# A two-layer hybrid diffusion step on one core: mLSTM decay matrices built with the value blocks, and the layer norm's residual on another engine, traced later, with the layer norm at higher priority

## The chip, the cores and the metric

The kernel runs on one core of one Trainium2 chip. The metric is device microseconds of one execution, the median of the runs shown; lower is better. The engines are named as in the profile: PE (TensorE; PEld is its weight load), DVE (VectorE), ACT (ScalarE), POOL (GpSimd) and SP (SyncE, which here only issues transfers).

## The reference

Two token streams of 128 tokens and 1024 channels, a context (s = 0) and a sample (s = 1), go through the same two layers. A layer is a half-step SwiGLU feed-forward, a mixer and another half-step feed-forward. Each of these six sub-layers ends in a layer norm over a residual sum:

```python
f1 = _swiglu(x * (1.0 + sc1) + sh1, ffn1_w_gate, ffn1_w_up, ffn1_w_down)
x = _layer_norm(alpha * x + 0.5 * g1 * f1, ln_g, ln_b)
y, new_st = _mixer(x * (1.0 + sc2) + sh2, st, l, p)
x = _layer_norm(alpha * x + g2 * y, ln_g, ln_b)
```

The mixer runs gated linear attention (GLA, 4 heads) and an mLSTM (4 heads), each forward and backward, and merges them. The part of the mLSTM that the change touches is the decay matrix of each direction and head, and the factor of the carried state:

```python
log_d = where(mask, cum[..., :, None] - cum[..., None, :] + ic[..., None, :], -inf)
m_t = maximum(cum + m, log_d.max(-1))
d = exp(log_d - m_t[..., None])
inter = exp(cum + m - m_t)
s = einsum('bhtd,bhsd->bhts', q, k) * d
```

## The kernel before

All weights are fp32 and stream once from HBM. A `Block` is one 128x512 result per stream; it is cut into units of up to four 128-row weight tiles. For each half unit a 128x1024 tile `raw` is loaded, ACT rounds it to `hi` (L303) and DVE forms `lo = raw - hi` (L304), and PE adds three products, `hi·xh`, `lo·xh` and `hi·xl` (L319 to L321). `raw` has six buffers, `hi` and `lo` seven each, so a half unit's `hi` can be made only when PE has used an older one.

The main loop (L1047) takes one unit a turn: it loads the next unit, consumes unit i for stream 0 and unit i - 2 for stream 1 (`LAG = 2`), and adds a few conditioning matmuls. A block's `pre` runs before its first matmul of a stream, its `post` after its last.

The program is traced in that order, and a scheduler of the kernel's framework fixes each engine's queue when the kernel is compiled. It goes through the program on a clock of its own, and on each engine takes, of the instructions that are ready there, the one traced first. `issue_after(ins)` puts instructions behind `ins` on its engine, and `high_priority(offset=n)` ranks instructions as if they had been traced n earlier. On the chip each queue then runs strictly in that order. Most large tiles share one pool, `s4`, of 21 slots; they take slots in the order of tracing, so a tile traced late can't be made before those ahead of it have had theirs.

At the end of a sub-layer `ln_half` (two per stream: `y = acc·gate`, `y = alpha·x + y`, statistics; L377 to L381) and `ln_finish` run: mean and variance (L392), `rstd` on DVE and a power on POOL (L386), the normalised `y` (L398), eight transposes on PE, the modulated `mf` on DVE and ACT (L352, L354), and its split into `xh` (ACT) and `xl` (DVE, L332), which the next sub-layer's first matmuls need. The residual stream itself, `x = y·g + b`, is four POOL instructions of 128x512 for each stream (L404, L405); it is next read at the end of the following sub-layer.

In the mixer, `chain` (L531) is called ahead of stream 1's first unit. It makes the gates' running maxima, stores them (`Gd`), loads them back as rows spread over all partitions (`Db`, four transfers of 256 KB, L583), and at once makes the factors `ib` (ACT, eight exponentials, L588) and the decay matrices of both streams (DVE, 16 instructions, L592; ACT, two exponentials of 128x1024, L594). They are first used by block `q0`, the blocks' order being `v0 v1 k0 n0 k1 n1 r0 q0 ...` of two units each.

Of the kernel before, what the change touches and what calls it, by code (L numbers as in the profile page):

```python
# [12 lines left out]
AF = mybir.ActivationFunctionType  # L13
ALU = mybir.AluOpType
# [3 lines left out]
D = 1024  # L18
KT = D // 128
# [8 lines left out]
C_GG, C_GM = 7216, 8240  # L28
LAG = 2
SLOTS = 21  # L30


@with_exitstack
def hybrid_step(ctx: ExitStack, tc: tile.TileContext, I, O, n_sub=6):
# [21 lines left out]
    def s4(name, shape, dt=F32):  # L56
        return s4_p.tile([128] + shape, dt, name=name, tag="s4")
# [219 lines left out]
    def add_block(b, step=4):  # L277
        k0 = 0
        while k0 < b.nk:
            n = min(step, b.nk - k0)  # L280
            units.append((b, k0, n, {}, phase[0]))
            k0 += n

    def load(u, part=None):
        b, k0, n, w, _ = u
        for h in range(0, n, 2):
            if part == 1:
                raw = w.pop("raw")
                split_w(raw, w, h)
                continue  # L290
            raw = raw_p.tile([128, 2, 512], F32, name="raw", tag="raw")
            for src, c0, nn in b.srcs:
                nc.sync.dma_start(raw[:, :, c0:c0 + nn],
                                  src[128 * (k0 + h):128 * (k0 + h + 2), :].rearrange("(k p) n -> p k n", p=128))
            if part == 0:
                w["raw"] = raw
            else:
                split_w(raw, w, h)
# [71 lines left out]
    def ln_half(s, n, acc, fac):  # L370
        if n == 0:
            yt[s] = s4("y", [D])
            bst[s] = sm("bst", 12)
        sl = slice(512 * n, 512 * n + 512)
        y = yt[s]
        if fac == 1.0:
            V.tensor_tensor(y[:, sl], acc, gbc[s][:, sl], ALU.mult)  # L377
        else:
            V.scalar_tensor_tensor(y[:, sl], acc, fac, gbc[s][:, sl], ALU.mult, ALU.mult)
        V.scalar_tensor_tensor(y[:, sl], x[s][:, sl], ALPHA, y[:, sl], ALU.mult, ALU.add)  # L380
        V.bn_stats(bst[s][:, 6 * n:6 * n + 6], y[:, sl])  # L381
# [7 lines left out]
    def ln_finish(s, l, sub):  # L389
        y = yt.pop(s)  # L390
        mv = sm("mv", 2)
        V.bn_aggr(mv, bst.pop(s).rearrange("p (a b) -> p a b", b=6))  # L392
        r = rstd_of("rstd", mv[:, 1:2], 1.0, LN_EPS)
        idx = l * 3 + sub
        if idx + 1 < n_sub:
            for n in range(2):
                sl = slice(512 * n, 512 * n + 512)
                V.tensor_scalar(y[:, sl], y[:, sl], mv[:, 0:1], r, ALU.subtract, ALU.mult)  # L398
        if idx + 1 < n_sub:
            l2, sub2 = divmod(idx + 1, 3)  # L400
            modulate(s, y, l2, sub2)
            for n in range(2):
                sl = slice(512 * n, 512 * n + 512)
                G.tensor_tensor(x[s][:, sl], y[:, sl], lnbc["g"][:, sl], ALU.mult)  # L404
                G.tensor_tensor(x[s][:, sl], x[s][:, sl], lnbc["b"][:, sl], ALU.add)  # L405
        else:
            for n in range(2):
                sl = slice(512 * n, 512 * n + 512)
                V.scalar_tensor_tensor(y[:, sl], y[:, sl], mv[:, 0:1], lnbc["g"][:, sl], ALU.subtract, ALU.mult)
                V.scalar_tensor_tensor(x[s][:, sl], y[:, sl], r, lnbc["b"][:, sl], ALU.mult, ALU.add)  # L410
                nc.sync.dma_start(O["y_prompt" if s == 0 else "y_sample"][0, :, sl], x[s][:, sl])


    def ffn(l, sub, wg, wu, wd):
        sg, hid = {}, {}

        def xin(s, k):
            return xh[s][:, k, :], xl[s][:, k, :]

        def hidden(s, h, j, nt):  # L420
            pt = ms("hT", [4, 128])
            for t in range(nt):
                T.transpose(pt[:, t, :], h[:, 128 * t:128 * (t + 1)], ident)  # L423
            ht = s4("hid", [2, 4, 128], F32R) if nt == 4 else hb_p.tile([128, 2, 2, 128], F32R, name="hidb", tag="hidb")
            hid[s, j] = ht
            split_fm(ht[:, 0, 0:nt, :], ht[:, 1, 0:nt, :], pt[:, 0:nt, :])

        def gate_post(s, acc):
            sg[s] = t2("sg", [512])
            A.activation(sg[s], acc, AF.Silu)  # L430

        def up_post(j):
            def f(s, acc):
                h = sg.pop(s)
                V.tensor_tensor(h, h, acc, ALU.mult)
                hidden(s, h, j, 4)
            return f

        def mix_post(s, acc):
            h = t2("sg", [256])  # L440
            A.activation(h, acc[:, 0:256], AF.Silu)
            V.tensor_tensor(h, h, acc[:, 256:512], ALU.mult)
            hidden(s, h, 5, 2)

        for j in range(5):
            sl = slice(512 * j, 512 * j + 512)
            step = 2 if j == 0 and l == 0 and sub == 0 else 4
            add_block(Block(KT, [(wg[:, sl], 0, 512)], xin, gate_post), step)
            add_block(Block(KT, [(wu[:, sl], 0, 512)], xin, up_post(j)), step)
            if step == 2:  # L450
                units[:] = [units[4 * (i % 2) + i // 2] for i in range(8)]
        add_block(Block(KT, [(wg[:, 2560:2816], 0, 256), (wu[:, 2560:2816], 256, 256)], xin, mix_post))

        def hin(s, k):
            t = hid[s, k // 4]
            return t[:, 0, k % 4, :], t[:, 1, k % 4, :]

        def down_post(n):
            def f(s, acc):
                ln_half(s, n, acc, 0.5)  # L460
                if n == 1:
                    ln_finish(s, l, sub)
            return f

        for n in range(2):
            add_block(Block(KF, [(wd[:, 512 * n:512 * n + 512], 0, 512)], hin, down_post(n),
                            pre=(lambda s: ln_prefetch(s, l, sub)) if n == 0 else None))


    def mixer(l):  # L470
# [60 lines left out]
        def chain():  # L531
# [44 lines left out]
            A.activation(en, mt, AF.Exp, scale=-1.0)  # L576
            gd = dr_p.tile([128, 128], F32, name="Gd", tag="Gd")
            nc.sync.dma_start(gd, Gr)
            for s in range(2):
                Db = st["D", s] = s4("Db", [2, 4, 128])  # L580
                for d in range(2):
                    r = 32 * (2 * s + d)
                    nc.sync.dma_start(Db[:, d], gd[r:r + 4, :].unsqueeze(0).to_broadcast([128, 4, 128]))  # L583
                if s == 1:
                    ib = st["ib"] = s4("ib", [2, 4, 128])
                    for d in range(2):
                        for h in range(4):
                            A.activation(ib[:, d, h, :], Db[:, d, h, :], AF.Exp, scale=-1.0,  # L588
                                         bias=m0bc[l][:, 4 * d + h:4 * d + h + 1])
                for d in range(2):  # L590
                    for h in range(4):
                        V.scalar_tensor_tensor(Db[:, d, h, :], Db[:, d, h, :], gpad[:, s, d, h:h + 1],  # L592
                                               mk[:, 6 + d, :], ALU.subtract, ALU.max)
                A.activation(Db, Db, AF.Exp, scale=-1.0)  # L594
            Q.dma_start(O["m"][0, l, 0:1, :], m4[127:128, 0, 0, :])
            Q.dma_start(O["m"][0, l, 1:2, :], m4[0:1, 1, 0, :])


        vg, on = {}, {}
# [165 lines left out]
        def vm_post(n):  # L765
            def f(s, acc):
                if n == 0:
                    vm[s] = s4("vm", [4, 257])
                    G.memset(vm[s][:, :, 256:257], 1.0)
                A.activation(vm[s][:, 2 * n:2 * n + 2, 0:256], acc.rearrange("p (a b) -> p a b", a=2), AF.Copy)  # L770
            return f
# [100 lines left out]
        def col(c, n=512):  # L872
            return [(W[:, c:c + n], 0, n)]
# [7 lines left out]
                            xin, gla_post(pr), pre=gla_pre(pr)))  # L881

        def b_n(n):
            add_block(Block(KT, col(C_VM + 512 * n), xin, vm_post(n)))

        def b_q(h):
            add_block(Block(KT, [(W[:, C_QKM + 256 * h:C_QKM + 256 * h + 256], 0, 256),
# [60 lines left out]

        def out_post(n):
            def f(s, acc):  # L950
                ln_half(s, n, acc, 1.0)
                if n == 1:
                    ln_finish(s, l, 1)
            return f

        for n in range(2):
# [90 lines left out]
    for i in range(s0, n + LAG):  # L1047
        ahead = units[i + 1] if i + 1 < n else None
        if ahead and not last(i - LAG):
            load(ahead)  # L1050
        if i < n:
            consume(0, units[i])
        if i - LAG >= s0:
            consume(1, units[i - LAG])
        if ahead and last(i - LAG):
            with tc.issue_after(fin["V", 0, 0]), tc.issue_after(fin["A", 0, 0]):
                load(ahead)
        if i < n:
            for a in due[i]:
                ada_unit(*a)  # L1060
# [87 lines left out]
```

## Time and profile before

| | us |
|---|---|
| median of 3 runs | 1630.68 (1630.48 to 1632.51) |
| the profiled execution | 1633.1 |
| its span, first to last instruction | 1631.2 |
| PE busy in the span | 1584.0 (97%) |
| DVE busy | 978.9 (60%) |
| ACT busy | 757.4 (46%) |
| POOL busy | 117.9 (7%) |
| mean granted clock of PE | 0.991 |

The profiled execution is 1.9 us longer than its span and 2.4 us longer than the median. Ends of matmuls are modelled, so a busy PE is not a PE at its peak; where PE shows idle time, it had nothing to do. The six sub-layers end at about 250, 640, 850, 1045, 1425 and 1623 us of the span.

### The profile page before, as it was taken

The numbers are of one execution on the slowest core, as the hardware profiler recorded it, in microseconds if no ns is written. First come the engines' busy times: TensorE is split into PE (matmuls) and PEld (weight loads), VectorE is DVE, ScalarE is ACT, GpSimd is POOL, SyncE is SP. The second block draws the span as 40 slices with busy tenths as digits, with TensorE's granted clock in tenths as the row PEclk, the third lists the DMA queues.
The fourth block names the chain that finished last, engine by engine and source line by source line (L and its number), as shares of the span: only waits on it lengthen the run. The fifth ranks groups of instructions, "written<-read, shape, count | busy, mean of one in ns | idle before, by whom it ended". The sixth has DMA issues, their size and how long they took to land.

```text
span 1631.2 us, 20327 instructions
## 1 busy us (share of the span) xinstructions
PE 1584.0 (97%) x7323; PEld 1192.0 (73%) x7323; DVE 978.9 (60%) x1607; ACT 757.4 (46%) x1096; POOL 117.9 (7%) x142
## 2 busy tenths in 40 slices
PE   7999999899999999999999999989999999999997
PEld 3676676677677677777777888767777777768886
DVE  3544458557666558645565555666577665765555
ACT  2443334555565534444444444355556554454441
POOL 2000004000000002100011000220000000120000
PEclk9999999999999999999999999999999999999999
DMA  9777876665775785666855667576556766756671
GB/s 325 250 266 258 309 232 210 207 215 171 256 232 182 272 284 167 216 218 205 282 189 157 181 182 246 164 214 212 182 183 195 252 193 233 217 161 182 181 236 65
DMA packets 195982, 350.20 MB, mean 215 GB/s; under 512 B 17516, under 2 KB 73596, under 8 KB 195880
## 3 DMA queue, kind: packets, MB, share of 16 engines
q1 hardware_dynamic: 195320, 348.68, 66.3%
q8 instruction: 58, 0.95, 0.2%
q0 software_dynamic: 384, 0.13, 0.1%
q14 instruction: 44, 0.36, 0.1%
q10 hardware_dynamic: 176, 0.07, 0.0%
HBM read 341.30 MB, written 7.54 MB: 214 GB/s over the span
## 4 chain that ended last, share of the span: by engine, by line
PE 57%; issue 30%; DVE 6%; DMA 3%; ACT 2%; POOL 1%; SPq 0%; DVEq 0%; POOLq 0%; ACTq 0%
PE acc L319 15%; PE acc L320 15%; PE acc L321 15%; PE adaps L167 3%; DVE lo L304 2%; DMA Db<-Gd 1%; PE cfin L846 1%; PE hT L423 1%; DVE xl L332 1%; DMA araw<-in_w_ada 1%; POOL rstd L386 1%; PE num L818 1%; PE num L821 1%; ACT hi L303 1%; PE rg L798 0%
## 5 line engine op out<-in xcount | busy, mean ns | idle before, releaser
L304 DVE TENSOR_TENSOR lo<-raw,hi 128x1024 fp32r<-128x1024 f32 x456 | 559.5, 1229 | 366.5 <-ACT hi L303 363.7
L303 ACT ACTIVATE hi<-raw 128x1024 fp32r<-128x1024 f32 x456 | 480.9, 1059 | 426.4 <-PE acc L321 394.9
L319 PE MATMUL acc<-hi,xh 128*128 128x512 f32 x1280 | 517.2, 406 | 12.7 <-ACT xh L330 7.0
L321 PE MATMUL acc<-hi,xl 128*128 128x512 f32 x1280 | 515.0, 403 | 5.6 <-DVE xl L332 5.4
L320 PE MATMUL acc<-lo,xh 128*128 128x512 f32 x1280 | 514.2, 402 | 2.8 <-DVE lo L304 2.8
L319 PEld LDWEIGHTS acc<-hi,xh 128*128 128x128 f32 x1280 | 242.1, 189 | 110.8 <-issue 27.9
L321 PEld LDWEIGHTS acc<-hi,xl 128*128 128x128 f32 x1280 | 243.0, 190 | 63.5 <-DVE xl L332 9.5
L320 PEld LDWEIGHTS acc<-lo,xh 128*128 128x128 f32 x1280 | 242.8, 190 | 59.0 <-DVE lo L304 7.4
L319 PE MATMUL acc<-hi,hid 128*128 128x512 f32 x320 | 127.0, 397 | 0.0
L320 PE MATMUL acc<-lo,hid 128*128 128x512 f32 x320 | 126.6, 396 | 0.0
L321 PE MATMUL acc<-hi,hid 128*128 128x512 f32 x320 | 126.4, 395 | 0.0
L167 PE MATMUL adaps<-araw,condp 128*32 128x512 f32 x512 | 78.7, 604 | 0.0
L319 PEld LDWEIGHTS acc<-hi,hid 128*128 128x128 f32 x320 | 60.1, 188 | 18.7 <-issue 3.4
L320 PEld LDWEIGHTS acc<-lo,hid 128*128 128x128 f32 x320 | 60.1, 188 | 14.4 <-issue 0.8
L321 PEld LDWEIGHTS acc<-hi,hid 128*128 128x128 f32 x320 | 60.2, 188 | 13.9
L386 POOL TENSOR_TENSOR rstd<-rstd,mhalf 128x1 f32<-128x1 f32 x12 | 13.9, 1158 | 777.0 <-DVE rstd L385 661.0
L330 ACT ACTIVATE hid<-hT 128x512 fp32r<-128x512 f32 x40 | 24.0, 599 | 85.8 <-PE hT L423 85.7
L319 PE MATMUL acc<-hi,oh 128*128 128x512 f32 x128 | 51.2, 400 | 0.0
L320 PE MATMUL acc<-lo,oh 128*128 128x512 f32 x128 | 51.2, 400 | 0.0
L321 PE MATMUL acc<-hi,ol 128*128 128x512 f32 x128 | 50.5, 395 | 0.0
L386 POOL TENSOR_TENSOR hr<-hr,mhalf 128x1 f32<-128x1 f32 x32 | 17.9, 560 | 422.5 <-DVE hr L385 362.9
L430 ACT ACTIVATE sg<-acc 128x512 f32<-128x512 f32 x40 | 23.9, 598 | 46.4 <-PE acc L321 46.4
(246 smaller groups left out, 1539.6 us busy)
## 6 DMA issues: line engine op xcount, KB each, us to landing
araw<-in_w_ada SPq DMA_DIRECT2D x128, 512.0 KB
raw<-in_w_in SPq DMA_DIRECT2D x96, 512.0 KB
raw<-in_ffn_w_down SPq DMA_DIRECT2D x88, 512.0 KB
raw<-in_ffn_w_gate SPq DMA_DIRECT2D x80, 512.0 KB
raw<-in_ffn_w_up SPq DMA_DIRECT2D x80, 512.0 KB
raw<-in_w_in SPq DMA_DIRECT2D x96, 256.0 KB
araw<-in_w_ada SPq DMA_DIRECT2D x32, 256.0 KB
raw<-in_w_br_gla SPq DMA_DIRECT2D x16, 512.0 KB
```

Source lines behind the costliest of these rows:

```text
L167: T.matmul(ps[32 * q:32 * q + 32, :], lhsT=condp[:, k, :], rhs=raw[q], start=(k == 0), stop=(k == KT - 1), tile_position=(0, 32 * q))
L303: A.activation(hi, raw, AF.Copy)
L304: V.tensor_tensor(lo, raw, hi.bitcast(F32), ALU.subtract)
L319: T.matmul(acc, lhsT=xh, rhs=wh, start=(k == 0), stop=False)
L320: T.matmul(acc, lhsT=xh, rhs=wl, start=False, stop=False)
L321: T.matmul(acc, lhsT=xl, rhs=wh, start=False, stop=(k == b.nk - 1))
L330: a = A.activation(dst_h, src, AF.Copy, scale=scale)
L332: v = V.tensor_tensor(dst_l, src, dst_h.bitcast(F32), ALU.subtract)
L386: G.tensor_tensor(r, r, mhalf[:, 0:1], ALU.pow)
L423: T.transpose(pt[:, t, :], h[:, 128 * t:128 * (t + 1)], ident)
L430: A.activation(sg[s], acc, AF.Silu)
L818: T.matmul(num, lhsT=sT[:, d, :], rhs=vh, start=True, stop=(s == 0))
```

## The change

There are two parts. In the mixer, `chain` keeps only the store of `Gd`; the loads of a stream's rows move to the `pre` of block `n0`, and `ib` and the decay matrices of that stream to the `pre` of block `n1`. At the ends of sub-layers, `ln_half` and `ln_finish` are traced with a priority 100 higher, and the residual becomes two DVE instructions of 128x1024 for each stream, traced at the end of the second turn after the one in which `ln_finish` ran and put behind the last `xl` of that stream on DVE's queue. The number and size of all other instructions stay.

```diff
+PRIO = 100
...
             modulate(s, y, l2, sub2)
-            for n in range(2):
-                sl = slice(512 * n, 512 * n + 512)
-                G.tensor_tensor(x[s][:, sl], y[:, sl], lnbc["g"][:, sl], ALU.mult)
-                G.tensor_tensor(x[s][:, sl], x[s][:, sl], lnbc["b"][:, sl], ALU.add)
+            later.append([3, s, y, lnbc["g"], lnbc["b"], fin["V", s, 1]])
...
+    later = []
+
+    def residuals():
+
+        for e in later:
+            e[0] -= 1
+        while later and later[0][0] <= 0:
+            _, s, y, g, b, behind = later.pop(0)
+            with tc.issue_after(behind):
+                V.tensor_tensor(x[s], y, g, ALU.mult)
+                V.tensor_tensor(x[s], x[s], b, ALU.add)
...
-                ln_half(s, n, acc, 0.5)
-                if n == 1:
-                    ln_finish(s, l, sub)
+                with tc.high_priority(offset=PRIO):
+                    ln_half(s, n, acc, 0.5)
+                    if n == 1:
+                        ln_finish(s, l, sub)
...
             nc.sync.dma_start(gd, Gr)
-            for s in range(2):
-                Db = st["D", s] = s4("Db", [2, 4, 128])
-                for d in range(2):
-                    r = 32 * (2 * s + d)
-                    nc.sync.dma_start(Db[:, d], gd[r:r + 4, :].unsqueeze(0).to_broadcast([128, 4, 128]))
...
+            st["gd"] = gd
...
+        def rows_load(s):
+            Db = st["D", s] = s4("Db", [2, 4, 128])
+            for d in range(2):
+                r = 32 * (2 * s + d)
+                nc.sync.dma_start(Db[:, d], st["gd"][r:r + 4, :].unsqueeze(0).to_broadcast([128, 4, 128]))
+
+        def decays(s):
+            mk, Db = st["mk"], st["D", s]
+            if s == 1:
+                ib = st["ib"] = s4("ib", [2, 4, 128])
                 for d in range(2):
                     for h in range(4):
+                        A.activation(ib[:, d, h, :], Db[:, d, h, :], AF.Exp, scale=-1.0,
+                                     bias=m0bc[l][:, 4 * d + h:4 * d + h + 1])
+            for d in range(2):
+                for h in range(4):
+                    V.scalar_tensor_tensor(Db[:, d, h, :], Db[:, d, h, :], gpad[:, s, d, h:h + 1],
+                                           mk[:, 6 + d, :], ALU.subtract, ALU.max)
+            A.activation(Db, Db, AF.Exp, scale=-1.0)
...
         def b_n(n):
-            add_block(Block(KT, col(C_VM + 512 * n), xin, vm_post(n)))
+            add_block(Block(KT, col(C_VM + 512 * n), xin, vm_post(n), pre=(rows_load, decays)[n]))
...
+        residuals()
         if i < n:
             for a in due[i]:
                 ada_unit(*a)
```

`out_post` of the mixer gets the same `high_priority` as `down_post`.

## Rows read from the trace of the kernel before

**Rows 1.** The page, part 1: busy time, share of the span, instructions.

```profile
PE 1584.0 (97%) x7323; PEld 1192.0 (73%) x7323; DVE 978.9 (60%) x1607; ACT 757.4 (46%) x1096; POOL 117.9 (7%) x142
```

**Rows 2.** Windows: stretch, length, busy us (instructions) by engine, granted clock, DMA share, GB/s.

```profile
250.00:275.00 25.00, 22.84 (x119) 15.73 (x118) 20.33 (x38) 10.96 (x19) 16.88 (x13) 1.00 0.69 225
295.00:300.00 5.00, 3.85 (x19) 2.84 (x17) 2.23 (x9) 0.56 (x2) 0.00 (x0) 1.00 0.96 219
300.00:305.00 5.00, 1.64 (x5) 1.30 (x6) 2.33 (x8) 5.00 (x12) 0.00 (x0) 0.89 0.73 281
305.00:310.00 5.00, 5.00 (x20) 3.25 (x18) 0.93 (x1) 3.83 (x9) 0.00 (x0) 0.77 0.00 0
385.00:400.00 15.00, 15.00 (x78) 12.14 (x78) 11.18 (x25) 10.22 (x16) 0.53 (x1) 1.00 0.46 142
635.00:660.00 25.00, 21.09 (x95) 15.51 (x94) 21.68 (x34) 13.55 (x20) 14.87 (x10) 1.00 0.48 149
850.00:855.00 5.00, 1.60 (x4) 0.84 (x5) 5.00 (x6) 4.96 (x8) 4.04 (x3) 0.84 0.14 53
855.00:860.00 5.00, 5.00 (x13) 3.84 (x13) 4.56 (x8) 0.25 (x1) 1.46 (x1) 0.50 0.43 110
860.00:865.00 5.00, 5.00 (x27) 4.26 (x26) 2.40 (x6) 1.88 (x4) 4.61 (x4) 0.98 0.58 208
1045.00:1070.00 25.00, 21.97 (x111) 15.61 (x110) 20.34 (x38) 10.48 (x19) 17.47 (x13) 1.00 0.55 185
1090.00:1095.00 5.00, 2.27 (x13) 1.62 (x12) 2.74 (x9) 2.31 (x6) 0.00 (x0) 1.00 1.02 199
1095.00:1100.00 5.00, 5.00 (x20) 4.05 (x19) 1.52 (x5) 4.41 (x10) 0.00 (x0) 0.66 1.05 381
1420.00:1445.00 25.00, 20.99 (x95) 15.46 (x94) 21.71 (x33) 13.37 (x20) 15.36 (x10) 1.00 0.46 147
```

**Rows 3.** Waits of 284:310 us: who waited for whom, total, times, longest.

```profile
ACT ib L588 <- DMA Db<-Gd: 5.5, 1, 5.5
...
PE acc L319 <- ACT vg L605: 4.5, 1, 4.5
```

**Rows 4.** Waits of 1080:1100 us.

```profile
ACT ib L588 <- DMA Db<-Gd: 2.9, 1, 2.9
PE argA L657 <- DVE lal L332: 2.7, 1, 2.7
```

**Rows 5.** Tile Db: duration ns min/median/max, first and last start, forms.

```profile
L592 DVE SCALAR_TENSOR_TENSOR Db<-Db,gpad,mk x32: 343/350/354, 294.8 to 1096.2; 128x128 f32<-128x128 f32 x32
L588 ACT ACTIVATE ib<-Db,m0bc x16: 385/387/402, 299.4 to 1095.8; 128x128 f32<-128x128 f32 x16
...
L594 ACT ACTIVATE Db<-Db x4: 1040/1050/1062, 300.6 to 1096.6; 128x1024 f32<-128x1024 f32 x4
```

**Rows 6.** Timeline of VectorE, 842:860 us: start, length, instruction, idle before.

```profile
844.60 1.21 DVE L304 TENSOR_TENSOR lo<-raw,hi 128x1024 fp32r<-128x1024 f32 x1
...
845.84 1.17 DVE L304 TENSOR_TENSOR lo<-raw,hi 128x1024 fp32r<-128x1024 f32 x1
...
851.22 1.69 DVE L380 SCALAR_TENSOR_TENSOR y<-x,y 128x512 f32<-128x512 f32 x1
852.83 1.76 DVE L332 TENSOR_TENSOR xl<-mf,xh 128x512 fp32r<-128x512 f32 x1
...
856.24 0.68 DVE L332 TENSOR_TENSOR xl<-mf,xh 128x512 fp32r<-128x512 f32 x1
```

**Rows 7.** Line L405 (residual on GpSimd): duration ns min/median/max.

```profile
L405 POOL TENSOR_TENSOR x<-x,lnbbc x20: 1272/1297/2253, 254.3 to 1443.7; 128x512 f32<-128x512 f32 x20
```

**Rows 8.** The page, part 5: instruction, count, busy us, mean ns, idle before it.

```profile
L304 DVE TENSOR_TENSOR lo<-raw,hi 128x1024 fp32r<-128x1024 f32 x456 | 559.5, 1229 | 366.5 <-ACT hi L303 363.7
```

**Rows 9.** Timeline of VectorE, 902:911 us, inside a feed-forward layer.

```profile
909.20 1.22 DVE L304 TENSOR_TENSOR lo<-raw,hi 128x1024 fp32r<-128x1024 f32 x1 [2.98 <-ACT hi L303]
```

**Rows 10.** Timeline of GpSimd, 0:4 us.

```profile
1.26 0.75 POOL L120 DMA_DIRECT2D m0bc<-in_state_mlstm_m  x1 [0.81 <-POOLq L1133]
```

More of the change, by code (lines that the diff above doesn't have):

```diff
@@ L578, in chain @@
             nc.sync.dma_start(gd, Gr)
-            for s in range(2):
-                Db = st["D", s] = s4("Db", [2, 4, 128])
-                for d in range(2):
-                    r = 32 * (2 * s + d)
-                    nc.sync.dma_start(Db[:, d], gd[r:r + 4, :].unsqueeze(0).to_broadcast([128, 4, 128]))
[L584 to L589, printed above, removed]
+            st["gd"] = gd
+            Q.dma_start(O["m"][0, l, 0:1, :], m4[127:128, 0, 0, :])
+            Q.dma_start(O["m"][0, l, 1:2, :], m4[0:1, 1, 0, :])
+        def rows_load(s):
[7 more added lines that the diff above has]
+                ib = st["ib"] = s4("ib", [2, 4, 128])
                 for d in range(2):
                     for h in range(4):
[L592 to L596, printed above, removed]
+                        A.activation(ib[:, d, h, :], Db[:, d, h, :], AF.Exp, scale=-1.0,
[5 more added lines that the diff above has]
+            A.activation(Db, Db, AF.Exp, scale=-1.0)
         vg, on = {}, {}
@@ L950, in f @@
             def f(s, acc):
-                ln_half(s, n, acc, 1.0)
-                if n == 1:
-                    ln_finish(s, l, 1)
+                with tc.high_priority(offset=PRIO):
+                    ln_half(s, n, acc, 1.0)
+                    if n == 1:
+                        ln_finish(s, l, 1)
             return f
```

## The prediction, made before the result was known

> **What bounds the kernel now.** I read the page's busy times first. PE is busy for 1584.0 of 1631.2 us [rows 1], so some 47 us are all that other engines can give back at PE's present work. Next I cut the span into windows to find where these 47 us lie. A part lies in the program's start and behind its last matmul, which the change doesn't touch. The rest stands in two kinds of place [rows 2], and between them PE has next to none. The reader should take two things from each window: its length less PE's busy time, and the granted clock, because a PE that runs at half clock counts as busy.
>
> The first kind is the start of each mixer. Layer 0 loses 1.15 us in 295 to 300 and 3.36 in 300 to 305; layer 1 loses 2.73 in 1090 to 1095 [rows 2]. Behind each the granted clock falls for a while from its upper level, 2.4 GHz, to the lower, 1.2: 0.89 and 0.77 over five us each are (0.11 + 0.23) x 5 = 1.7 us of lost work, and 0.66 in layer 1 is again 1.7 us [rows 2]. The waits say why. ACT sat 5.5 us in front of its first `ib` exponential until the rows `Db` had landed, and PE waited 4.5 us for a copy of `acc` that stood behind it in ACT's queue [rows 3]. In layer 1 ACT waited 2.9 us for the same transfer, and PE 2.7 us for a GLA split that stood behind the decay work on DVE [rows 4]. The values waited for are needed first by block `q0`, many units later. So these are waits in front of work that isn't urgent.
>
> The second kind is the ends of sub-layers. PE idles 2.16, 3.91, 3.40, 3.03 and 4.01 us in the five stretches, 16.5 in all, and at 850 to 865 the clock costs (0.16 + 0.50 + 0.02) x 5 = 3.4 us more [rows 2]. There DVE is the full engine: 20.3 to 21.7 of 25 us, and 5.00 of 5 at 850 [rows 2]. The timeline shows two things in its queue that lengthen the layer norm's chain. Two weight splits `lo` of 1.2 us stand between the statistics and `rstd` [rows 6]. And DVE instructions with two operands in SBUF are slow while POOL computes the residual: `y` took 1.69 us and the first `xl` 1.76, where the second `xl`, of the same size, took 0.68 once POOL was done [rows 6].
>
> **The change part by part, decay matrices.** What leaves the mixer's start is, for each layer, four row transfers, eight `ib` exponentials of 0.39, 16 DVE instructions of 0.35 and two exponentials of 1.05 [rows 5]. The wait in front of them goes with them, and I book it whole: 1.15 + 3.36 + 1.7 + 2.73 + 1.7 = 10.6 us. The lower bound is nothing, if another late instruction is found behind the wait.
>
> The work comes back in front of `n0` and `n1`. The row loads pass the weight loads of `v1` and `k0` on SP's queue; `Gd` has long landed, so they hold up nothing there, and they have two blocks' time to land. If that cover were gone, the 5.5 us of rows 3 would stand again. Stream 1's part of the arithmetic is 8 x 0.39 + 1.05 = 4.2 us of ACT and 8 x 0.35 = 2.8 us of DVE, and it falls in a stretch like 385 to 400. There ACT has 15 - 10.2 = 4.8 us free and DVE 3.8, with PE at 15.00 of 15 [rows 2]. It fits, but barely, and what stands behind it in ACT's queue is the `hi` of coming weights. Bounds: 0 to 7 us a layer (all of it on the path). I take 1.5 a layer, nearer to "it fits": 3 us. That `ib` isn't simply made as early as before, which a scheduler that takes whatever is ready could do, I read from the pool: its slot of `s4` comes after those of the GLA tiles of `k0` and `k1`. Net: 7.6 us gained.
>
> **Layer norm.** POOL loses 40 instructions of about 1.3 us [rows 7]. POOL is 7% busy [rows 1] and its own time is on no path, so this counts only through DVE: about 1.0 us for each slowed instruction on the chain (1.69 and 1.76 against 0.68). The priority lets the statistics and `rstd` pass the two `lo` ahead of them, 2.4 us in each chain where they stand (1.21 + 1.17) [rows 6]; mixer ends have fewer. So 3 to 4 us come out of a chain whose stretch loses 2 to 4 us of PE. I don't book it all. The `lo` displaced must still run before the next matmuls, the scheduler will put one of 1.2 us into the short wait for POOL's power, and the chain of matmul, transpose, `mf`, `xh` and `xl` remains. I take half of the idle time, 8.3 us, and half of the clock loss, 1.7 us, as the clock's fall came after an idle stretch that may now be too short for it. Bounds: 0, and 16.5 + 3.4 = 19.9.
>
> A rule of the Trainium skill bears on the size of this ("SBUF — State Buffer", section "SBUF: two separate sides"): VectorE and GpSimd share one pair of ports as a lock, so whichever comes second waits for the whole instruction of the other. By it a slowed instruction would lose up to one POOL instruction, 1.3 us, where the rows show 1.0; with one or two such on each of ten chains that would be 3 to 6 us more to win. I keep to the rows.
>
> The residual now costs DVE five ends x two streams x two instructions. Their shape is that of `lo`, two SBUF operands of 128x1024, mean 1.23 us [rows 8], so 24.6 us in all. The cover is DVE's own idle time: 366 us stand in front of the `lo` alone [rows 8], and a feed-forward layer has gaps of 2.98 us, in which both fit [rows 9]. Queued behind a residual are the `lo` of the next weights; PE waits if they are later than their slack. Bounds: 0 to 24.6. Most should fall into gaps, so I take 1.5. The priority also lifts the layer norm's first halves: 12 times three instructions of 0.68 us go ahead of a `lo`, 24.5 us if each were on the path, 0 if they end in a gap as in rows 9; 2.0 us fit in 2.98, so I take 0.5.
>
> The sum: 7.6 + 8.3 + 1.7 - 1.5 - 0.5 = 15.6 us. On the profiled execution, 1631.2 of span and 1.9 around it, that is 1633.1 - 15.6 = 1617.5. The median shown is 2.4 us lower, so 1630.7 - 15.6 = 1615.1: I predict 1615.
>
> **The rivals.** *Decay only.* The layer norm's halves cancel: the chain gets shorter, but `lo` and residuals run in its gaps and PE waits for weights instead of `xl`. For it: DVE is at 5.00 of 5 at 850 [rows 2], and less work isn't given to it but more. Against it: the slowed instructions are measured. Time: 1630.7 - 7.6 = 1623.
>
> *Nearly all.* The chain fits behind the other stream's matmuls, 80% of the 16.5 us and all of the clock loss go: with 1 us for the moved decay work and 2 for residuals and first halves, as in the forecast, 1630.7 - 10.6 + 1 - 13.2 - 3.4 + 2 = 1606.5, and 1603.5 if those were free too.
>
> *The decay part doesn't do what it says.* The order is the scheduler's: it issues what is ready, however late it was traced; POOL's load of `m0bc`, traced behind the first eight units, went out at 1.26 us [rows 10]. If the rows get slots early, `ib` stands in ACT's queue as before and the wait only changes place: the forecast without its 7.6 us, 1615.1 + 7.6 = 1622.7. Against it: `ib` waits for a slot of `s4` behind many tiles.
>
> *Slower.* Residuals become the bound. Place: DVE right after a sub-layer's end, where it is already at 20.3 to 21.7 of 25 us [rows 2]. Each residual holds the queue for 1.23 us ahead of an `xl`, a GLA split or a `lo` that PE wants; all of them on the path cost 24.6 us in place of my 1.5: 1615.1 + 23.1 = 1638.2. It decides for "slower" once it takes 15.6 + 1.5 = 17.1 us, about 70% of the residuals' time. The Trainium skill would have it so ("Perfetto Trace Analysis", section "Optimizing Scalar/DVE Operations"): with VectorE saturated, work may be better off on GpSimd; the same section doubts that between these two it helps. The trace agrees that DVE is full at these ends; no row shows it full for longer.
>
> *No change.* Both moves give back what they win: about 1630.
>
> **How the numbers follow.** The forecast has a chance of 0.53, with a range of its own of 1609 to 1621; decay only 0.15, nearly all 0.11, the decay part moved 0.05, slower 0.10, no change 0.06. What the measurement can tell from no change is about 0.2%, 3.3 us. So faster is 0.53 + 0.15 + 0.11 + 0.05 = 0.84, same 0.06, slower 0.10. The range of 1603 to 1626 takes in the first four cases with the bounds of their terms and leaves out the last two.
>
> **What would show it.** Right, step by step: no wait of ACT for `Db` in the mixers, PE above 4.8 of 5 us where it was 1.64 and 2.27, and the clock at 1.00 behind it; `ib` and L592 found between the GLA heads of `k1`, with PE still full there; no L404 and L405 on POOL and `xl` at 0.68 us throughout; `rstd` directly behind the statistics; residuals of 1.23 us on DVE with no new wait of PE for `lo`; and idle time in the five stretches of about 8 us in place of 16.5. The prediction fails if PE's waits for `lo` (L320) grow by several us behind the ends, if the wait for `Db` turns up elsewhere, or if new idle time appears around `n1` and `r0`, where the decay work now stands.

## The result, and the profile after

The changed kernel takes 1613.51 us (median; 1611.61 to 1617.74), the kernel before 1630.58 in the same comparison: ratio 0.9897, 95% interval 0.9874 to 0.992. The forecast was 1615. The profiled execution's span is 1615.9 us, 15.3 less than before. The page's busy times, as in [rows 1]:

```profile
PE 1576.5 (98%) x7323; PEld 1190.9 (74%) x7323; DVE 985.8 (61%) x1627; ACT 757.1 (47%) x1096; POOL 55.6 (3%) x102
```

Half of the 15.3 us is idle time of PE (47.2 us before, 1615.9 - 1576.5 = 39.4 now); the other half is less *busy* time, 1584.0 to 1576.5, though PE runs the same 7323 matmuls. The prediction spoke only of idle time and clock. All that is read of the clock below is one execution's: the one shown is the slowest of the changed kernel's four (mean clock 0.992 beside 0.994, 0.995 and 0.995), and the kernel before ran at 0.989 to 0.997 over 17 executions.

Windows of the changed kernel; columns as in [rows 2]. The ends now come up to 17 us earlier, so the stretches are moved with them.

```profile
248.00:273.00 25.00, 24.20 (x127) 17.27 (x126) 21.71 (x42) 12.02 (x20) 4.50 (x5) 1.00 0.70 225
300.00:305.00 5.00, 5.00 (x29) 3.21 (x28) 3.63 (x8) 2.52 (x6) 0.57 (x1) 1.00 0.77 218
310.00:315.00 5.00, 4.10 (x18) 3.02 (x17) 3.87 (x12) 4.61 (x7) 0.60 (x2) 1.00 0.68 253
385.00:400.00 15.00, 14.82 (x78) 10.57 (x77) 10.51 (x28) 6.53 (x12) 0.55 (x1) 1.00 0.70 213
625.00:650.00 25.00, 21.32 (x94) 15.84 (x93) 21.72 (x36) 13.16 (x20) 2.94 (x2) 0.98 0.48 147
834.00:859.00 25.00, 22.99 (x99) 17.66 (x98) 21.80 (x35) 12.44 (x20) 2.01 (x2) 0.93 0.44 132
1032.00:1057.00 25.00, 24.14 (x123) 17.74 (x122) 22.72 (x43) 12.43 (x20) 4.38 (x5) 1.00 0.61 187
1090.00:1095.00 5.00, 4.17 (x26) 2.35 (x24) 2.12 (x4) 2.46 (x4) 0.27 (x1) 1.00 0.91 286
1095.00:1100.00 5.00, 3.35 (x9) 2.68 (x10) 3.59 (x12) 0.75 (x3) 0.64 (x2) 0.60 0.71 241
1100.00:1105.00 5.00, 5.00 (x18) 3.94 (x17) 1.01 (x4) 3.40 (x5) 0.00 (x0) 0.72 0.28 72
1405.00:1430.00 25.00, 21.35 (x90) 15.83 (x89) 21.51 (x34) 12.33 (x20) 2.08 (x2) 0.94 0.42 127
```

Three things are to be seen.

The five ends lose 0.80 + 3.68 + 2.01 + 0.86 + 3.65 = 11.0 us of PE in place of 16.5, and the gain sits at the ends into a mixer (2.16 and 3.03 to 0.80 and 0.86) and between the feed-forward layers (3.40 to 2.01). The ends out of a mixer are nearly as they were.

In this execution the clock gave nothing back at the ends: (0.02 + 0.07 + 0.06) x 25 = 3.75 us of lost work in these windows, and 1.1 more as the fall at the first of the three goes on behind 650 us (0.78 in 650 to 655). That is 4.9 us in place of 3.4. It now falls at each of three ends, where before it fell at one, and for longer.

Layer 0's mixer start is mended (300 to 305 full, clock 1.00; 0.90 us idle at 310 to 315). Layer 1's isn't: 0.83 + 1.65 us idle, and (0.40 + 0.28) x 5 = 3.4 us of clock. Waits of 1080 to 1100 us, where [rows 4] had ACT waiting for `Db`:

```profile
DVE Db L610 <- DMA Db<-Gd: 2.7, 1, 2.7
PE gla_o L728 <- DVE attT L725: 2.5, 1, 2.5
```

The transfer waited for is the same, but DVE waits for it now, and stands. Timeline of DVE, 1092 to 1103 us: start, length, instruction, idle time before it.

```profile
1092.15 0.30 DVE L724 COPY_PREDICATED attT<-mk,att 128x128 f32<-128x128 uint32 x1
1095.12 0.35 DVE L610 SCALAR_TENSOR_TENSOR Db<-Db,gpad,mk 128x128 f32<-128x128 f32 x1 [2.67 <-DMA Db<-Gd]
1095.39 0.29 DVE L724 COPY_PREDICATED attT<-mk,att 128x128 f32<-128x128 uint32 x1
...
1096.31 0.28 DVE L725 TENSOR_TENSOR attT<-attT,mc 128x128 f32<-128x128 f32 x1
```

The second L724 is the GLA's mask, which needs nothing of `Db`. It stood 2.7 us behind the first decay instruction in the queue, and PE's `gla_o` behind it.

DVE stands for the same transfer in layer 0, and longer; PE lost only the 0.90 us there. Timeline of DVE, 302 to 313 us:

```profile
310.36 1.14 DVE L610 SCALAR_TENSOR_TENSOR Db<-Db,gpad,mk 128x128 f32<-128x128 f32 x4 [3.06 <-DMA Db<-Gd]
```

These are the decays of stream 0. Those of stream 1 and `ib` run where the prediction had them, among the GLA heads: `ib` from 373.6 us and L610 from 377.7 in layer 0, and up to 1170 in layer 1.

At the ends, the timeline of DVE, 832 to 847 us, answers to [rows 6]:

```profile
834.08 0.69 DVE L382 BATCH_NORM_STATS2 bst<-y 128x6 f32<-128x512 f32 x1
834.69 1.21 DVE L305 TENSOR_TENSOR lo<-raw,hi 128x1024 fp32r<-128x1024 f32 x1
835.81 0.20 DVE L393 BATCH_NORM_AGGREGATE mv<-bst 128x2 f32<-128x12 f32 x1
835.93 1.18 DVE L305 TENSOR_TENSOR lo<-raw,hi 128x1024 fp32r<-128x1024 f32 x1
837.02 0.15 DVE L386 TENSOR_SCALAR rstd<-mv 128x1 f32<-128x1 f32 x1
...
841.91 0.68 DVE L333 TENSOR_TENSOR xl<-mf,xh 128x512 fp32r<-128x512 f32 x1
...
846.25 0.15 DVE L386 TENSOR_SCALAR rstd<-mv 128x1 f32<-128x1 f32 x1
846.31 1.22 DVE L420 TENSOR_TENSOR x<-y,lngbc 128x1024 f32<-128x1024 f32 x1
```

The two `lo` still stand between stream 0's statistics and its `rstd`, priority or not. `xl` takes 0.68 us. And a residual (L420) of stream 0 has slipped into stream 1's chain, behind its `rstd`.

### The profile page after: what moved, and what is told of

Read it like the earlier page. It is cut to its first block, busy times and chain, and to the rows that moved or that the text cites. A ratio compares the mean times of both kernels' runs of the same rounds, so it can differ in the third digit from the quotient of the medians.

```text
span 1615.9 us, 20299 instructions
## 1 busy us (share of the span) xinstructions
PE 1576.5 (98%) x7323; PEld 1190.9 (74%) x7323; DVE 985.8 (61%) x1627; ACT 757.1 (47%) x1096; POOL 55.6 (3%) x102
## 4 chain that ended last, share of the span: by engine, by line
PE 81%; issue 8%; DVE 5%; DMA 2%; ACT 2%; POOL 1%; SPq 0%; DVEq 0%; POOLq 0%; ACTq 0%
PE acc L320 23%; PE acc L322 22%; PE acc L321 22%; PE adaps L168 3%; DVE lo L305 2%; DMA araw<-in_w_ada 1%; PE hT L433 1%; PE num L837 1%; ACT hi L304 1%; PE num L834 1%; PE gps L531 1%; PE zps L630 0%; DMA Db<-Gd 0%; PE rg L814 0%; PE gla_o L728 0%
## 5 line engine op out<-in xcount | busy, mean ns | idle before, releaser
L305 DVE TENSOR_TENSOR lo<-raw,hi 128x1024 fp32r<-128x1024 f32 x456 | 557.0, 1223 | 355.6 <-ACT hi L304 347.3
L168 PE MATMUL adaps<-araw,condp 128*32 128x512 f32 x512 | 74.2, 605 | 0.7 <-DMA araw<-in_w_ada 0.7
L333 DVE TENSOR_TENSOR hid<-hT,hid 128x512 fp32r<-128x512 f32 x40 | 27.5, 691 | 28.0 <-ACT hid L331 28.0
```

The lines of the kernel that those rows point to most:

```text
L168: T.matmul(ps[32 * q:32 * q + 32, :], lhsT=condp[:, k, :], rhs=raw[q], start=(k == 0), stop=(k == KT - 1), tile_position=(0, 32 * q))
L305: V.tensor_tensor(lo, raw, hi.bitcast(F32), ALU.subtract)
L333: v = V.tensor_tensor(dst_l, src, dst_h.bitcast(F32), ALU.subtract)
```

## The experiments

The theories. *Port*: the layer norm gains because GpSimd no longer reads SBUF beside DVE's two-operand instructions. *Queue*: it gains because the priority takes its instructions past the `lo`. *Layer norm only*: the decay part merely moves its wait. Twelve kernels were timed in three groups; each group has its own runs of the kernel before (medians 1628.8, 1628.3 and 1627.4 us, and 1630.6 beside the whole change), so ratios are what is compared between groups.

**The parts alone and in pairs.** *decays_only*: residual on GpSimd, no priority.

```diff
-            later.append([3, s, y, lnbc["g"], lnbc["b"], fin["V", s, 1]])
+            for n in range(2):
+                sl = slice(512 * n, 512 * n + 512)
+                G.tensor_tensor(x[s][:, sl], y[:, sl], lnbc["g"][:, sl], ALU.mult)
+                G.tensor_tensor(x[s][:, sl], x[s][:, sl], lnbc["b"][:, sl], ALU.add)
...
-                with tc.high_priority(offset=PRIO):
-                    ln_half(s, n, acc, 0.5)
...
+                ln_half(s, n, acc, 0.5)
```

> Only the decay part; the layer norm's half is undone (residual on GpSimd, no priority). Three theories of the 17 us that the change gained. Port theory: the layer norm's share (some 10 us) comes from taking the residual off GpSimd, and the decay part gives 5 to 8 us, since the row wait comes back in part in layer 1: 1623 to 1626. Queue theory (the prediction's step): the priority gives most of the layer norm's share, the decay part 7.6: 1623. Layer-norm-only theory: the decay wait has only moved, 1629 to 1631.

Measured: 1623.45 us, ratio 0.9966 (0.9954 to 0.9979). *decays_priority* has the first hunk alone (residual on GpSimd, with the priority):

> Decay part and priority, residual still on GpSimd. Port theory: the two-operand instructions of VectorE stay slow (xl 1.5 to 1.8 us beside GpSimd), so little more than the decay part: 1621 to 1625. Queue theory: 2.4 us out of each chain whose lo stand in the way: 1614 to 1618.

Measured: 1621.29 us, 0.9954 (0.9941 to 0.9968). *decays_residual* has the second hunk alone (residual on VectorE, no priority):

> Decay part and residual on VectorE, without the higher priority. Port theory: nearly all of the gain stays, 1614 to 1618. Queue theory: without the priority the two lo stay ahead of rstd and the residuals only add work to VectorE: 1622 to 1626.

Measured: 1611.70 us, 0.9895 (0.9879 to 0.9912), which is the whole change's 0.9897, and by the time 2 us below *port*'s range. *ln_only* is the whole change with all lines of the decay part as in the kernel before:

> Priority and residual on VectorE, decay matrices where they were. Port and queue theory: the changed kernel without its 6 to 8 us of the decay part, 1619 to 1622, with the wait of ScalarE for Db of 3 to 6 us per layer back. Layer-norm-only theory: 1613 to 1615.

Measured: 1621.24 us, 0.9952 (0.9939 to 0.9965). *residual_only* takes the priority out of that too:

> The kernel before with the residuals on VectorE and nothing else: decays where they were, no priority. If GpSimd's reads are what made the layer norm slow, this alone takes back what the layer norm's two changes together took (0.9952, 1621.2 us), perhaps a little more since the priority is absent at the ends out of a mixer: 1619 to 1622 us. If the priority is needed for the residuals' move to pay, 1624 to 1630 us.

Measured: 1623.37 us, 0.9979 (0.9966 to 0.9991). By the time that is between the two expectations; on the 1628.8 us of the group from which they were worked out the ratio gives 1625.4, inside the second.

With the decays moved, the residual's place is worth 0.71% (0.9966 to 0.9895) and the priority nothing that these runs can tell, with the residual on either engine. *Queue* falls there, as it does in the timeline above. Without the decays moved, the residual's place is worth 0.21% and the priority a further 0.27% (0.9979 to 0.9952, intervals just apart). *Layer norm only* falls too: the decay part alone is worth 0.34%.

**GpSimd reading again, at the ends.** Work is added to *decays_residual* whose result nothing reads:

```diff
             modulate(s, y, l2, sub2)
+            for n in range(8):
+                sl = slice(256 * (n % 4), 256 * (n % 4) + 256)
+                G.tensor_tensor(junkp, y[:, sl], lnbc["g"][:, sl], ALU.mult)
```

> Decays moved and residuals on VectorE, without the priority (1611.7 us), plus eight two-operand GpSimd multiplications of 128 x 256 on each stream's normalised rows, ahead of nothing that is computed: only work is added, its result is never read. By the theory that GpSimd's reads hold up VectorE's two-operand instructions, the casts to xl and the lo beside them go back from 0.7 towards 1.5 us, some 8 of them at each of five ends, and the time returns to 1619 to 1624 us. By the rival, that the gain came from the residuals' place in the queue and not from GpSimd being free, nothing waits for the added work and the time stays within 1609 to 1614 us.

Measured: 1626.41 us, 0.9987 (0.9978 to 0.9996). Nearly the whole gain is gone, the decay part's included, and more than *port* had said: the kernel is slower than *decays_only* (0.9966), but GpSimd also reads for 90.5 us here, where the residual took 61.0, and DVE has the residual as well. Groups of DVE by shape (count, busy us, mean ns, idle before): the 20 large `xl` of the kernel before, *decays_residual* and *gpsimd_reads*, in this order.

```profile
L332 DVE TENSOR_TENSOR xl<-mf,xh 128x512 fp32r<-128x512 f32 x20 | 24.4, 1245 | 6.5 <-ACT xh L330 6.5
```

```profile
L333 DVE TENSOR_TENSOR xl<-mf,xh 128x512 fp32r<-128x512 f32 x20 | 13.2, 687 | 5.5 <-ACT xh L331 5.4
```

```profile
L334 DVE TENSOR_TENSOR xl<-mf,xh 128x512 fp32r<-128x512 f32 x20 | 21.9, 1122 | 5.4 <-ACT xh L332 5.4
```

The instruction is the same and the tile is the same; only GpSimd's work beside it differs. Split by whether a multiplication ran at the same time, the 18 that met one took a mean of 1.17 us and the 2 others 0.68; in the kernel before, 13 met a residual instruction and took 1.55, 7 didn't and took 0.68. In *gpsimd_reads* the `lo` stay at a mean of 1.23 us, since few of the 456 meet GpSimd; the 14 that do take 1.43.

A rival is GpSimd's queue: the power for `rstd` could stand behind the added work. The trace rules it out. GpSimd was idle before the power in all 12 cases, and DVE waited 5.1 us for it in the ten chains, where it waited 5.2 in *decays_residual*.

**GpSimd writing only.** Sixteen `G.memset(junkp, 0.0)` of 128x256 in the place of the eight multiplications:

> The same kernel with sixteen GpSimd fills of 128 x 256 in the place of the eight multiplications: GpSimd is as busy, but reads nothing. If it is GpSimd's reading that slows VectorE, the casts stay at 0.7 us and the time at 1609 to 1614 us; if a busy GpSimd is enough, whatever it does, the casts rise and the time is 1618 to 1624 us.

Measured: 1616.4 us, 0.9928 (0.9915 to 0.994), and the experiment missed its place. Nothing holds a fill back, so the scheduler put all 160 into the program's first 75 us:

```profile
L406 POOL MEMSET junkp<- x160: 302/311/330, 8.6 to 75.4; 128x256 f32 x160
```

The time says nothing of the ends, then; the first end starts at 254.8 us in place of 251.3, so 3.5 us were lost before it. But GpSimd was 49.9 of 66.8 us busy with fills in that stretch, and DVE's two-operand work ran beside it. Groups of DVE in 8.6 to 75.4 us of *gpsimd_writes*:

```profile
L306 DVE TENSOR_TENSOR lo<-raw,hi 128x1024 fp32r<-128x1024 f32 x15 | 17.9, 1222 | 4.2 <-ACT hi L305 4.2
L334 DVE TENSOR_TENSOR xl<-mf,xh 128x256 fp32r<-128x256 f32 x8 | 3.4, 426 | 7.8 <-ACT xh L332 7.8
```

Without the fills the same groups take 1223 and 426 ns. The 14 `lo` of the whole run that met a fill took 1.222 us, the 442 others 1.223. A GpSimd that is busy but only writes slowed neither group; at the ends themselves this wasn't tried.

**The residuals out of stream 1's chain.** *decays_residual* with

```diff
-            with tc.issue_after(behind):
+            with tc.issue_after(fin["V", 1, 1]):
```

> Decays moved and residuals on VectorE, without the priority (1611.7 us), with the residuals put behind the last cast of the second stream instead of behind the first units, so that none stands between that stream's statistics and its casts. If the residuals of 1.2 us that slipped into the second stream's chain are what is left of the wait, each of five ends gives back about one to two of them: 1602 to 1607 us. If VectorE fills those places with the next lo anyway, or the residuals now crowd the first units, 1610 to 1614 us.

Measured: 1613.94 us, 0.9913 (0.99 to 0.9927): no gain, by the second expectation. The stages say why; they stand in the table below.

**The decays' VectorE work held back.** The whole change with

```diff
+            with tc.issue_after(last_lo[0]):
                 for d in range(2):
                     for h in range(4):
                         V.scalar_tensor_tensor(Db[:, d, h, :], ...
```

where `last_lo[0]` is the last L305 traced before it.

> The whole change (1613.5 us) with one alteration: VectorE's work on the decays stands behind the last lo traced before it, so that it can't be issued while its load is still under way. In the changed kernel VectorE stood 2.7 us for that load in layer 1, TensorE 2.5 us behind it, and a stretch at half clock followed. If that wait is what keeps the decay part from its full gain, it goes, and its clock with it: 1607 to 1611 us. If the wait only moves on to whoever comes next (ScalarE's exponential of the decays, or the mixer's own first use), 1612 to 1615 us.

Measured: 1610.22 us, 0.9897 (0.9881 to 0.9912). In the trace the wait is gone and so is the clock's fall. Windows of *decays_held*:

```profile
1090.00:1095.00 5.00, 5.00 (x23) 3.41 (x23) 1.77 (x3) 2.60 (x7) 0.60 (x2) 1.00 0.87 294
1095.00:1100.00 5.00, 5.00 (x29) 3.87 (x27) 1.94 (x3) 3.27 (x6) 0.00 (x0) 1.00 0.57 180
1100.00:1105.00 5.00, 5.00 (x29) 4.03 (x28) 2.96 (x10) 3.62 (x8) 0.00 (x0) 1.00 0.65 202
```

Its profiled span is 1605.9 us, 10 less than the whole change's, but at a clock of 0.996 beside 0.992, and the ratio of medians is the same. By the time it is in the first range, by the ratio (1613.8 on the whole change's 1630.6) in the second. So the trace bears out that the wait goes, and no gain in time is shown. *decays_held_no_priority* is the same edit on *decays_residual*:

> Decays moved, residuals on VectorE, decays' VectorE work behind the last lo, no priority at all. Without the priority the kernel took 1611.7 us and had no such wait in layer 1. If the wait for the load was all that the holding mends, nothing is to be had here: 1610 to 1613 us, and with the priority the held kernel is then the faster one. If the priority costs more at the ends than it gives (stream 1's first transpose 15.6 us behind stream 0's at the ends out of a mixer with it, 14.5 without), this one is 1606 to 1609 us and faster than the held kernel with the priority.

Measured: 1611.17 us, 0.9906 (0.9891 to 0.9922): nothing to be had, as the first expectation had it. In *decays_residual* DVE did wait for `Db` in layer 0, 2.6 us, but PE was not idle behind it. Whether the held kernel with the priority is faster, the intervals leave open.

**All three together.** *into_mixers_only*: decays held, residuals held, and the priority only where a mixer follows:

```diff
-                with tc.high_priority(offset=PRIO):
+                with tc.high_priority(offset=PRIO if sub == 0 else 0):
```

> All parts with three alterations: the priority only for the layer norms that lead into a mixer, the residuals behind the second stream's last cast, the decays' VectorE work behind the last traced lo of the FFN. Where the priority shortened the distance between the streams' first transposes (11.3 to 9.3 us at the two ends into a mixer) it stays, where it lengthened it (14.5 to 15.6 us) it goes: 4 us of distance, of which TensorE's idle time takes perhaps half. With the held residuals 1602 to 1608 us. If distance between the streams is not what TensorE waits for any more, or the held decays wait for their load behind all that VectorE does, 1610 to 1615 us.

Measured: 1606.43 us (1605.89 to 1606.93), 0.9867 (0.9853 to 0.988), the fastest of all. Windows of two ends and of layer 1's mixer start:

```profile
621.00:646.00 25.00, 23.12 (x105) 17.50 (x104) 20.88 (x37) 13.55 (x20) 2.93 (x2) 1.00 0.55 168
829.00:854.00 25.00, 22.78 (x103) 17.00 (x102) 20.52 (x34) 12.53 (x20) 2.01 (x2) 1.00 0.46 138
1089.00:1094.00 5.00, 5.00 (x26) 4.08 (x25) 1.99 (x7) 1.95 (x6) 0.60 (x2) 1.00 0.71 210
1094.00:1099.00 5.00, 5.00 (x24) 4.04 (x23) 3.10 (x4) 3.70 (x7) 0.00 (x0) 1.00 0.95 346
```

The end out of layer 0's mixer loses 1.88 us where the whole change lost 3.68, and the clock falls at none of the five ends. *mixers_residual_free* is the same without the holding of the residuals:

> The fastest version so far (0.9867 of the kernel before: priority into the mixers only, residuals held behind the second stream's casts, decays held) without the holding of the residuals. If the held residuals carry part of it, the ratio goes back to 0.988 to 0.990 (1609 to 1612 us). If the priority's place and the held decays carry it, it stays at 0.986 to 0.988 (1605 to 1608 us): holding the residuals alone, without the other two, gave nothing that could be told (0.9913 beside 0.9895).

Measured: 1610.4 us, 0.99 (0.9884 to 0.9916): the held residuals carry about 0.33% here, though alone they carried nothing. The two ratios come from different groups and their intervals are just apart.

**The stages.** From the records of PE: the first transpose of stream 0 (`xT`, L349) marks each end; a stage runs from one mark to the next, the first from the span's start, the last to its end. The right column is how far stream 1's first transpose stands behind stream 0's, at the end into layer 0's mixer, the end out of it, and between the feed-forward layers. All in us.

| kernel | first | mixer 0 | FFN | FFN | mixer 1 | last | distance of the streams |
|---|---|---|---|---|---|---|---|
| before | 251.6 | 387.2 | 209.6 | 198.6 | 376.4 | 207.9 | 12.9, 16.5, 14.2 |
| whole change | 250.0 | 378.4 | 210.0 | 196.0 | 371.9 | 209.5 | 9.4, 15.6, 11.4 |
| decays_only | 250.4 | 385.1 | 211.1 | 198.5 | 371.3 | 208.4 | 14.2, 17.8, 14.3 |
| decays_priority | 250.1 | 379.7 | 210.4 | 198.4 | 371.4 | 208.0 | 10.8, 16.2, 14.1 |
| residual_only | 249.3 | 384.5 | 209.8 | 194.7 | 373.8 | 209.2 | 11.4, 14.5, 10.2 |
| ln_only | 249.9 | 382.7 | 210.2 | 194.7 | 373.8 | 208.2 | 9.4, 15.6, 10.2 |
| decays_residual | 251.3 | 378.0 | 209.4 | 195.4 | 366.8 | 208.8 | 11.4, 14.5, 10.2 |
| gpsimd_reads | 249.9 | 381.9 | 211.9 | 198.7 | 372.8 | 211.5 | 12.8, 16.1, 13.2 |
| residual_held | 249.4 | 381.3 | 207.1 | 195.3 | 371.7 | 205.9 | 11.4, 14.5, 10.2 |
| decays_held | 249.2 | 377.1 | 208.5 | 196.1 | 367.1 | 208.0 | 9.4, 15.6, 11.4 |
| into_mixers_only | 248.7 | 377.9 | 206.4 | 195.2 | 369.9 | 206.0 | 9.4, 14.5, 10.2 |

The distance shows what each part does to the chain: without the priority, moving the residual shortens it at every end, by 1.5 to 4.1 us; the priority shortens it by 2 to 3.4 us into a mixer and, with the residual on DVE, lengthens it by 1.1 out of one. Holding the residuals shortens the stages behind a mixer's end by 2.3 and 3.0 us, of which some 1.7 each is the clock: it fell there in the execution of *decays_residual* (0.76 in 646 to 653 us, 0.79 in 1417 to 1425) and not in that of *residual_held*; *residual_held* then loses 3.3 and 4.9 in the mixers.

The mixers hold something that no theory had. PE's busy time for the conditioning matmuls (L167 before, L168 else) in mixer 1, windows of that line alone; the kernel before, the whole change, and *residual_held*:

```profile
1046.90:1423.30 376.40, 21.20 (x128) 1.00 0.65 207
```

```profile
1034.50:1406.40 371.90, 17.05 (x128) 0.99 0.64 209
```

```profile
1033.10:1404.70 371.60, 21.20 (x128) 1.00 0.66 210
```

The same 128 matmuls take 4.2 us less of PE in the whole change, and in *decays_residual* too; in *residual_held*, *ln_only*, *residual_only* and *into_mixers_only* they take 21.20 as before. So most of the 4.9 us that *residual_held* loses in mixer 1 are these, and so are 2.7 of the 3.3 in mixer 0, where 192 of them take 27.65 us in *decays_residual* and 30.34 in *residual_held*.

## Why the prediction was right, point by point

The time was right to 1.5 us, and that is in part luck: two mis-sized terms and a windfall nearly cancel. Of the 15.3 us between the profiled spans, the terms that the prediction named give 7.8 (3.8 at the mixer starts, 5.5 of idle time at the ends, -1.5 of clock there).

**Decay part: 7.6 forecast; alone 0.34%, 5.5 us (interval 3.4 to 7.5), and 0.55%, 9 us, on top of the layer norm's part.** The mechanism held: ACT no longer waits for `Db` in front of urgent work, and where the decays stayed, as in *residual_only*, the wait stayed, ACT for `Db` 4.3 us. The step that failed in part is the cover, "they have two blocks' time to land", and with it "I book it whole". The prediction gave a reason that `ib` would stay in front of `n1`, its slot in `s4`; it gave none for DVE's L610, which overwrites `Db` and needs no new slot. The queue has stream 0's L610 so early that it waits for its load, at 310.4 and 1095.1 us, where *decays_held* has it at 340.3 and 1118.3. So the cover was never used: DVE stood 3.06 us in layer 0 and 2.67 in layer 1, and in layer 1 that brought 2.5 us of PE and 3.4 of clock. To this extent the rival "the decay part doesn't do what it says" was right, and the sign "if the wait for `Db` turns up elsewhere" was met. Idle time and clock at the mixer starts came to 0.90 + 0.83 + 1.65 + 3.4 = 6.8 us in place of 10.6. That *decays_held* removes it shows the cause: the queue's order, not the transfer's time. In *decays_only* it was layer 0 where PE paid. Waits of 310 to 330 us there:

```profile
PE argA L673 <- ACT lah L331: 2.6, 1, 2.6
DVE Db L612 <- DMA Db<-Gd: 2.2, 1, 2.2
```

So what PE loses by the wait depends on what else shifts the queues by a few us. The 3 us for the moved arithmetic were too much: in 370 to 385 and 1160 to 1175 us of the changed kernel, where stream 1's part of it now runs, PE is full:

```profile
370.00:385.00 15.00, 15.00 (x83) 12.63 (x82) 10.73 (x35) 11.52 (x24) 0.66 (x1) 1.00 0.57 196
1160.00:1175.00 15.00, 15.00 (x83) 11.58 (x81) 12.42 (x35) 11.93 (x24) 0.66 (x1) 1.00 0.56 175
```

**Layer norm, one step wrong.** "The priority lets the statistics and `rstd` pass the two `lo`" failed. The timeline has the same order as [rows 6]: the first `lo` starts at 834.69 while the last statistics still run, the second at 835.93 while their aggregate does. Each time the next instruction of the chain wasn't ready, and the scheduler gave the engine the next `lo`, as far as the chip's times stand for those of its clock. A rank decides between instructions that are ready; it keeps no engine free for one that soon will be. What the priority does do is bring stream 1's chain forward at ends into a mixer, by 2 us of distance.

**Layer norm, the step that carried it.** "About 1.0 us for each slowed instruction" was right in kind: `xl` fell from a mean of 1.245 to 0.686 us (0.87 for each that had met a residual instruction), and *gpsimd_reads* brings back the long casts, the distances and the time, with the residual on DVE all the while. The Trainium skill says so in "SBUF — State Buffer", section "Who interferes with whom": a VectorE instruction with two SBUF inputs contends with a GpSimd instruction that reads SBUF, not with one that only writes it. The runs agree with both halves, the second by the fills beside `lo` and `xl` (1222 and 426 ns, and 1223 and 426 without).

**Layer norm, the sizes.** 8.0 us were forecast net; measured were 0.48%, 7.8 us, alone and 0.69%, 11.2 us, on top of the decay part. In the trace, half of the idle time at the ends, 8.3, measured 16.5 - 11.0 = 5.5 us. Half of the clock loss, 1.7, measured less than nothing, 3.4 to 4.9, in the execution shown. Against that stands a saving that the sum didn't have: conditioning matmuls, 4.2 us in mixer 1. Of the other 3.3 us by which PE's busy time fell, 2.6 lie in the first stage (238.9 to 236.3 us): the clock of its first 60 us was 0.91 in the one execution and 0.97 in the other. None of the moved work stands there, so this isn't counted as the change's gain.

**Residuals on VectorE: 1.5 us forecast.** They are not all hidden, as 846.31 in the timeline shows. Holding them behind stream 1's casts was worth 0.33%, 5.4 us, in one setting and nothing in another. As holding them also lengthened the conditioning matmuls, and part of the difference was clock, the term itself stays open, between nothing and some 5 us. The rival "slower", 1638, needed 17 of the 24.6 us on the path; no run comes near it. The Trainium skill's advice for a saturated VectorE, which the prediction weighed ("Perfetto Trace Analysis", section "Optimizing Scalar/DVE Operations"), isn't borne out here, though the doubt that it adds for these two engines is: DVE is full at these ends, and the move to it paid.

**Open.** *decays_only* and *residual_only* add up to 0.55%, together they give 1.05%. Part of it is the conditioning matmuls, which got shorter only in kernels with the decays moved, and part the wait in layer 0 of *decays_only*; a run that fixes the place of either by hand wasn't made. Nor is it settled why the priority is worth 0.27% without the decay part and nothing with it (the two ratios behind the 0.27% come from different groups).

## What to carry to other kernels

Look for an engine off the critical path that reads beside a critical one: GpSimd was 7% busy, and its residual still nearly doubled the time of instructions that TensorE waited for; moving it to the busier engine was worth 0.21% by itself and 0.71% once the decays were out of the way. When work is moved out of an urgent place, move its wait too: put the first instruction that needs the transfer behind something late in the queue, since a scheduler that takes it early makes everything behind it wait; a place late in the program text isn't enough. And read a gain stage by stage even when the total is right, because here a returned wait and a windfall hid each other, and the clock of a single execution moved the profile by several us.

## What the runs showed of the hardware that was not expected

GpSimd suffers as well: the added multiplications of 128x256 took between 0.72 and 2.11 us, for one and the same instruction. The 59 that ran beside a DVE instruction with two operands in SBUF took a mean of 1.25 us, the 21 others 0.80. And PE's cost of the same conditioning matmuls, four of 32 columns each whose starts can lie about 6 ns apart, isn't fixed. Of the 127 steps from one start to the next in mixer 1, 88 are about nothing in the kernel before and 96 in the changed one; of the others, just over half are 0.43 to 0.45 us. There, in the changed kernel, none of the 32 groups of four is broken up; in the kernel before 8 are, three of them by matmuls of the GLA or the state (L700, L846) between the second and the third. So it is the order in PE's queue that differs; why the scheduler broke up the groups wasn't tried by itself.
